# A gated product transposed in 32 x 32 blocks on VectorE and put in place by DMA copies, with three gate tiles ahead of the first branch

## The chip, the cores and the metric

The kernel runs on one core of one Trainium2 chip. The metric is device microseconds of one execution, the median of three runs. The engines are called PE (matrix products), DVE (VectorE), ACT (ScalarE), POOL (GpSimd) and SP (SyncE, which here only issues DMAs). ACT and POOL issue DMAs too; an engine that issues a DMA, or waits to issue it, does nothing else meanwhile.

## The reference

A decoder block on 512 tokens of 1024 channels in float32: two mixers side by side, merged by gates, then a feed-forward layer. Cut to what matters here:

```python
u, v_g, q, k, v, q_idx, k_idx, w_idx, gates = split_cols(h @ w_in, IN_SIZES)
y_a = gelu(u) * (einsum('gts,bcsgd->bctgd', tril(w_s), layernorm(gelu(v_g))) + b_s)   # 512 x 512
y_b = dsa_attention(rope(q), rope(k), v, ...)      # 8 heads of 64, the best 128 keys of each query
g = sigmoid(gates)                                 # 2 branches x 1024 channels
merged = g[0] * (y_a @ w_out_a) + g[1] * (y_b @ w_out_b)
x = x + merged @ w_o
x = x + square(relu(rmsnorm(x) @ w_ff_in)) @ w_ff_out
```

`y_a`, the gated product, comes out with tokens on the partitions. The product with `w_out_a` needs its channels there. That is the transposition of this change.

## The kernel before

**Products.** Each float32 product is three matmuls of a faster format: a value is split into a high half, which ACT writes (L51), and a low half, which DVE writes as the difference (L52; POOL for the weight tiles 3 to 23). `gemm` (L158 to L160) then multiplies low by high, high by low and high by high. A step of `gemm` is these three matmuls of 512 columns. One output tile of 128 channels takes 24 matmuls where the inner length is 1024, and 12 where it is 512.

**Weights.** Weight tiles of 512 KB are numbered in the order of use. Tile n arrives in `wr` (two buffers; loaded from SP's queue for n of 24 and more, L118), ACT makes `wh` of it and DVE `wl` (three buffers each). The load of tile n + 2 can start once `wl` of tile n is done. Tile 24 is that of gb0 before and after.

**Order.** The program collects steps of matmuls in a list `todo`, and `fill(n)` takes n of them to stand between work that has to wait for other engines. The scheduler then fixes the order on each engine. No instruction passes another on its engine.

**Around the change.** PE runs the k projection of the first four heads, the spatial gate `sg` (L575 to L577; DVE makes `u`, the gated product, from it at L578), the q projection `q0` in two tiles, one tile of the second gate `gb0`, and then the eight tiles `oa0` to `oa7` of the first branch, which are y_a times w_out_a. Among the last twelve matmuls of q0 stand 16 transposes of 128 x 128 by PE, in four groups `yt0` to `yt3`; ACT copies each group out as `yaTh` and DVE makes `yaTl`:

```python
b = bank(f"yt{g}", "pa")
for c in range(NT):
    tc.keep_in_program_order(PE.transpose(b[:, c * P:(c + 1) * P], u[:, c, g * P:(g + 1) * P], ident))
ACT.activation(yaT[0][:, g], b, AF.Copy)
DVE.tensor_tensor(yaT[1][:, g], b, f32(yaT[0][:, g]), op=ALU.subtract)
```

Meanwhile POOL issues the copies that put k, then q, head by head into `kq` (L368), 64 KB each; the heads' scores read them.

**Attention.** A head has four blocks of 128 queries. For each block PE makes the scores `at` (L639, L640); DVE masks and reduces them (L643); ACT takes exp (L646); DVE takes the reciprocal and normalises `p` (L651, L652); PE transposes it into `pt` (L658); ACT and DVE split that into `pth` and `ptl` (L661, L662). After the fourth block PE multiplies by the values, `pv` (L670). Between these steps `fill` puts branch tiles, k and q projections and gate tiles: `gb1` among the first heads, and `gb2` to `gb7` with the q projection among the last four. When these are used up, the scheduler takes matmuls of the second branch, `ob` (y_b times w_out_b), forward as far as the halves of y_b of the earlier heads allow. The evacuation of a gate tile, `zb`, is DVE's (L602).

Of the kernel before, what the change touches and what calls it, by code (L numbers as in the profile page):

```python
# [12 lines left out]
AF = mybir.ActivationFunctionType  # L13
ALU = mybir.AluOpType

P = 128
S = 512
D = 1024
KD = D // P
NT = S // P  # L20
# [13 lines left out]
def hybrid_block_kernel(ctx: ExitStack, tc: tile.TileContext, A: dict, out: bass.AP):  # L34
    nc = tc.nc
    ACT, DVE, POOL, PE = nc.scalar, nc.vector, nc.gpsimd, nc.tensor
# [7 lines left out]
    def bank(name, tag="ps"):  # L44
        return ps.tile([P, 512], F32, tag=tag, bufs=4, name=name)

    def f32(ap):
        return ap.bitcast(F32)

    def split(hi, lo, src, eng=None):  # L50
        ACT.activation(hi, src, AF.Copy)  # L51
        (eng or DVE).tensor_tensor(lo, src, f32(hi), op=ALU.subtract)  # L52


    def unit(tag, dt, name):
# [3 lines left out]
    def half(tag, bufs, name):  # L59
        pool, dt = (G, F32) if tag == "yb" else (E, FR)  # L60
        return pool.tile([P, 4, S], dt, tag=tag, bufs=bufs, name=name)
# [15 lines left out]
    todo, due = [], []  # L77
# [10 lines left out]
    def fill(n):  # L88
        while n > 0 and todo:
            try:  # L90
                next(todo[0])
                n -= 1
                tick()
            except StopIteration:
                todo.pop(0)
# [56 lines left out]
    def gemm(dst, get, ah, al, evac, lag=1, t0=0):  # L152

        wh, wl, n = get()
        K = len(ah)
        for k in range(K):
            bh, bl = ah[k][:, t0:], al[k][:, t0:]
            PE.matmul(dst, wl[:, k], bh, start=(k == 0), stop=False)  # L158
            PE.matmul(dst, wh[:, k], bl, start=False, stop=False)  # L159
            PE.matmul(dst, wh[:, k], bh, start=False, stop=(k == K - 1))  # L160
            if k == 0 and n is not None:
                w_ahead(n)
            if k == K - 1:
                later(evac, lag)
            yield

    def one(src):
        n = w_plan(src)

        def get():  # L170
            return *w_get(n, P), n
        return get
# [16 lines left out]
    hTh = [G.tile([P, S], FR, tag="hTh", bufs=KD, name=f"hTh{k}") for k in range(KD)]  # L189
    hTl = [G.tile([P, S], FR, tag="hTl", bufs=KD, name=f"hTl{k}") for k in range(KD)]  # L190
# [10 lines left out]
    ident = G.tile([P, P], F32, name="ident")  # L201
# [14 lines left out]
    W_GA = [one(A["wt"][12 + m]) for m in range(KD)]  # L216
    W_K0 = [one(A["wt"][n]) for n in (4, 5)]
    W_Q0 = [one(A["wt"][n]) for n in (8, 9)]
    W_GB = [one(A["wt"][20])]
    W_OA = [g for m in range(4) for g in pair(A["woa"][m])]  # L220
    W_GB += [one(A["wt"][21])]
    W_K1 = [one(A["wt"][n]) for n in (6, 7)]
    W_Q1 = [one(A["wt"][n]) for n in (10, 11)]
    W_GB += [one(A["wt"][20 + m]) for m in range(2, KD)]
    W_OB = [g for m in range(4) for g in pair(A["wob"][m])]
    W_O = [one(A["wo"][m]) for m in range(KD)]
    NG = 8
# [13 lines left out]
    for t in raw2:  # L241
        t = f32(t.rearrange("p a b -> p (a b)"))
        raw += [t[:, i * NA:(i + 1) * NA] for i in range(3)]
    hl = []
    for k in range(KD):
# [5 lines left out]
        elif k < 6:  # L251
            t = E.tile([P, 13, P], FR, tag="pt", bufs=2, name=f"wa{k}").rearrange("p a b -> p (a b)")
# [77 lines left out]
    for j in range(NT):  # L330
        rj = rstd[:, j:j + 1]
        for n in range(2):
            src = acc[j][n][:, :256].rearrange("p (h d) -> p h d", d=64)
# [7 lines left out]
    def rope(xy, T, name, t0):  # L341


        for n in range(2):
            a, b = tmp(f"{name}_a{n}")[:, t0:], tmp(f"{name}_b{n}")[:, t0:]
            DVE.tensor_tensor(a, xy[n], cosR[:, t0:], op=ALU.mult)
            DVE.tensor_tensor(b, xy[1 - n], sinR[:, t0:], op=ALU.mult)
            DVE.tensor_tensor(a, a, b, op=ALU.subtract if n == 0 else ALU.add)
            if name == "k0":
                DVE.tensor_copy(T[n], a)  # L350
                DVE.tensor_tensor(T[2 + n], a, f32(T[n]), op=ALU.subtract)
            else:
                split(T[n], T[2 + n], a)

    def rope_tiles(gets, name, done, t0=0):
        xy = [bank(f"{name}{n}")[:, t0:] for n in range(2)]

        def finish():
            t = [unit("T", FR, f"{name}_T{c}") for c in range(2)]
            T = [t[c][:, d, t0:] for c in range(2) for d in range(2)]  # L360
            rope(xy, T, name, t0)
            done(T)
        for n in range(2):
            yield from gemm(xy[n], gets[n], hTh, hTl, finish if n else (lambda: None), t0=t0)

    def restack(dst, T, hh, order, eng=nc.sync):
        for c, o in enumerate(order):
# [44 lines left out]
    for n in range(2):  # L412
        b = bank(f"kti{n}", "pa")
# [7 lines left out]
    u, vg = None, None  # L421
# [55 lines left out]
    mA, mAs = [], eight("mA")  # L477
# [90 lines left out]
    fill(12)  # L568
    u = dst_uv["u"]
    vgh, vgl = vghl  # L570
    yaT = [half("ybt", 2, f"yaT{c}") for c in "hl"]
    for g in range(4):
        b = bank(f"sg{g}", "pa")
        c = slice(g * P, (g + 1) * P)
# [4 lines left out]
                                 u[:, :, c], op0=ALU.add, op1=ALU.mult)  # L579
    fill(4)  # L580
    todo.append(rope_tiles(W_Q0, "q0", q_done))
    fill(11)
    for g in range(4):
        fill(1)
        b = bank(f"yt{g}", "pa")
        for c in range(NT):
            tc.keep_in_program_order(PE.transpose(b[:, c * P:(c + 1) * P], u[:, c, g * P:(g + 1) * P], ident))
        ACT.activation(yaT[0][:, g], b, AF.Copy)
        DVE.tensor_tensor(yaT[1][:, g], b, f32(yaT[0][:, g]), op=ALU.subtract)
    while todo:  # L590
        fill(8)

# [2 lines left out]
    def gate_b(m):  # L595
        b = bank(f"gb{m}")

        def evac():
            if m % 4 == 0:
                z1t.append(half("yb", 2, f"zb{m}"))  # L600
            z = z1t[-1][:, m % 4]
            DVE.tensor_tensor(z, b, R, op=ALU.mult)  # L602
            z1.append(z)
        yield from gemm(b, W_GB[m], hTh, hTl, evac)

    def branch_a(m):
        b = bank(f"oa{m}")

        def evac():
            DVE.tensor_tensor(mA[m], b, mA[m], op=ALU.mult)  # L610
        yield from gemm(b, W_OA[m], [yaT[0][:, k] for k in range(4)], [yaT[1][:, k] for k in range(4)], evac)


    todo.append(gate_b(0))
    for m in range(KD):
        todo.append(branch_a(m))
    fill(32)


    START = (0, 1, 2, 2)  # L620
# [82 lines left out]
                b.last = i == NT - 1  # L703
                advance(b, n)

    todo.append(gate_b(1))
    heads(0, (0, 1), (6, 7))
    todo.append(rope_tiles(W_K1, "k1", lambda T: ybs.__setitem__("KT", T)))
    heads(0, (2, 3), (6, 7))
# [5 lines left out]
    flush()  # L715
    k_done(ybs["KT"])
    todo.append(rope_tiles(W_Q1, "q1", q_done))
    todo.extend(gate_b(m) for m in range(2, KD))
    fill(27)
    heads(1, range(4), (2, 0))  # L720
    advance(None, (2, 2))
# [364 lines left out]
def _col_tiles(w, cols):  # L1086

    k = w.shape[0] // P
    t = w[:, cols].reshape(k, P, -1, P)
    return np.ascontiguousarray(t.transpose(2, 1, 0, 3)).reshape(-1, P, k * P)  # L1090
# [11 lines left out]
def _layout(x, norm1_g, w_in, w_s, b_s, sgu_ln_g, sgu_ln_b, w_out_a, w_out_b, w_o,  # L1102
            norm2_g, w_ff_in, w_ff_out, norm_f_g):
    c = np.ascontiguousarray
    x = np.asarray(x)[0]
    w = np.asarray(w_in)[0]
    cos, sin = _tables()
    k = KD
    a = {}
    a["xT"] = c(x.T.reshape(k, P, S).transpose(1, 0, 2))  # L1110
    a["xn"] = c(x.reshape(NT, P, D).transpose(1, 0, 2))
    g1 = np.asarray(norm1_g)[0].reshape(k, P).T
    a["x0"] = c(np.concatenate([g1, np.zeros_like(g1), a["xT"][:, 0]], axis=1))

    rows = np.arange(D).reshape(4, KD, 32).transpose(1, 0, 2).reshape(-1)
    a["xr"] = c(x.T[rows].reshape(k, P, S).transpose(1, 0, 2))
    a["g2"] = c(np.asarray(norm2_g)[0][rows].reshape(k, P).T)
    a["gf"] = c(np.asarray(norm_f_g).reshape(1, D))
    a["wa"] = c(np.concatenate([w[:, 2048:2560], w[:, 3072:3144]], axis=1).reshape(k, P, 584).transpose(1, 0, 2))
    cols = _rope_cols(2560) + _rope_cols(1536) + _rope_cols(1024) + list(range(3144, 5192))  # L1120
    a["wt"] = _col_tiles(w, cols)
    a["wuv"] = c(w[:, :1024].reshape(4, 2, P, 2, S).transpose(3, 0, 2, 1, 4)).reshape(8, P, 2 * S)
    a["ws"] = c(np.asarray(w_s)[0].transpose(2, 0, 1))
    a["bs"] = c(np.asarray(b_s)[0].T)
    a["lng"] = c(np.asarray(sgu_ln_g).reshape(1, S))
    a["lnb"] = c(np.asarray(sgu_ln_b).reshape(1, S))

    def pairs(t):
        n, p, f = t.shape
        return c(t.reshape(n // 2, 2, p, f).transpose(0, 2, 1, 3)).reshape(n // 2, p, 2 * f)  # L1130

    a["woa"] = pairs(_col_tiles(np.asarray(w_out_a)[0], slice(None)))
    a["wob"] = pairs(_col_tiles(np.asarray(w_out_b)[0], slice(None)))
    a["wo"] = _col_tiles(np.asarray(w_o)[0], rows)
    a["f1"] = _col_tiles(np.asarray(w_ff_in)[0][rows], slice(None))
    f2 = np.asarray(w_ff_out)[0].reshape(16, 2, P, 2, S)
    a["f2"] = c(f2[14:].transpose(0, 3, 2, 1, 4)).reshape(4, P, 2 * S)
    a["f2p"] = c(f2[:14].transpose(0, 2, 1, 3, 4)).reshape(14, P, 4 * S)
    a["cs"] = c(np.stack([np.tile(cos.T, (4, 1)), np.tile(sin.T, (4, 1))], axis=1))
    a["csn"] = c(np.stack([cos, sin]).reshape(2, NT, P, 32).transpose(2, 0, 1, 3))  # L1140
    return a
# [17 lines left out]
```

## Time and profile before

| | |
|---|---|
| median of three runs | 693.05 us (692.77, 693.05, 693.35) |
| the profiled execution: time / span | 693.35 / 691.6 us |
| PE busy | 683.3 us, 99% |
| DVE busy | 549.1 us, 79% |
| ACT busy | 341.0 us, 49% |
| POOL busy | 136.5 us, 20% |
| granted clock of PE, mean | 0.998 of full speed |

The span runs from the first to the last instruction. Matmuls overlap in PE's pipeline: the profile gives each a duration of 0.39 us for 512 columns, while the next one starts some 0.23 us after it. So a timeline of PE is read by starts.

### The profile page before, as it was taken

The numbers are of one execution on the slowest core, as the hardware profiler recorded it, in microseconds if no ns is written. First come the engines' busy times: TensorE is split into PE (matmuls) and PEld (weight loads), VectorE is DVE, ScalarE is ACT, GpSimd is POOL, SyncE is SP. The second block draws the span as 40 slices with busy tenths as digits, with TensorE's granted clock in tenths as the row PEclk, the third lists the DMA queues.
The fourth block names the chain that finished last, engine by engine and source line by source line (L and its number), as shares of the span: only waits on it lengthen the run. The fifth ranks groups of instructions, "written<-read, shape, count | busy, mean of one in ns | idle before, by whom it ended". The sixth has DMA issues, their size and how long they took to land.

```text
span 691.6 us, 8980 instructions
## 1 busy us (share of the span) xinstructions
PE 683.3 (99%) x3206; PEld 572.9 (83%) x3206; DVE 549.1 (79%) x1013; ACT 341.0 (49%) x593; POOL 136.5 (20%) x178
## 2 busy tenths in 40 slices
PE   8999999999999999999999999999999999999996
PEld 8998888888888888788888888888888888888885
DVE  5584999999767877878558756978788797878996
ACT  6644644432345545573337765357462645546143
POOL 0044347862730850000027000000000000000001
PEclk9999999999999999999999999999999999999999
DMA  8736232322951662224458332232333214133023
GB/s 322 254 112 194 66 98 83 102 91 62 252 144 62 160 171 67 104 79 136 138 185 234 100 122 91 78 137 61 126 118 122 69 66 171 61 122 123 0 62 121
DMA packets 26844, 84.12 MB, mean 122 GB/s; under 512 B 5168, under 2 KB 6832, under 8 KB 24752
## 3 DMA queue, kind: packets, MB, share of 16 engines
q1 hardware_dynamic: 16944, 48.38, 22.2%
q10 hardware_dynamic: 5760, 26.78, 11.2%
q0 software_dynamic: 4096, 8.40, 4.7%
q8 instruction: 25, 0.41, 0.2%
q14 instruction: 19, 0.16, 0.1%
HBM read 71.48 MB, written 2.10 MB: 106 GB/s over the span
## 4 chain that ended last, share of the span: by engine, by line
PE 97%; DMA 1%; DVE 0%; ACT 0%; issue 0%; SPq 0%; POOLq 0%; POOL 0%
PE f L159 8%; PE f L158 8%; PE f L160 8%; PE pp L917 6%; PE pp L918 6%; PE pp L919 6%; PE va L297 3%; PE gb L160 2%; PE gb L159 2%; PE gb L158 2%; PE wo L159 2%; PE ga L159 2%; PE ga L158 2%; PE wo L160 2%; PE wo L158 2%; PE ga L160 2%
## 5 line engine op out<-in xcount | busy, mean ns | idle before, releaser
L51 ACT ACTIVATE wh<-wr 128x1024 fp32r<-128x1024 f32 x88 | 92.7, 1055 | 74.6 <-issue 18.0
L52 DVE TENSOR_TENSOR wl<-wr,wh 128x1024 fp32r<-128x1024 f32 x67 | 81.3, 1216 | 30.4 <-ACT wh L51 30.4
L158 PE MATMUL f<-h2h,wl 128*128 128x512 f32 x256 | 99.6, 389 | 0.0
L159 PE MATMUL f<-h2l,wh 128*128 128x512 f32 x256 | 99.6, 389 | 0.0
L160 PE MATMUL f<-h2h,wh 128*128 128x512 f32 x256 | 99.6, 389 | 0.0
L51 ACT ACTIVATE u<-w2r 128x512 fp32r<-128x512 f32 x98 | 59.0, 626 | 74.7 <-DVE w2r L848 28.1
L918 PE MATMUL pp<-u,fp 128*128 128x512 f32 x196 | 76.2, 389 | 0.0
L919 PE MATMUL pp<-u,fp 128*128 128x512 f32 x196 | 76.2, 389 | 0.0
L52 DVE TENSOR_TENSOR u<-w2r,u 128x512 fp32r<-128x512 f32 x98 | 64.1, 684 | 11.3 <-ACT u L51 11.3
L917 PE MATMUL pp<-u,fp 128*128 128x512 f32 x196 | 72.0, 389 | 0.0
L929 DVE TENSOR_TENSOR P<-pp,P 128x512 f32<-128x512 f32 x84 | 54.4, 683 | 16.6 <-PE pp L919 16.6
L52 POOL TENSOR_TENSOR wl<-wr,wh 128x1024 fp32r<-128x1024 f32 x21 | 52.6, 2504 | 47.5 <-ACT wh L51 45.7
L1014 POOL TENSOR_TENSOR fss<-fss,mhalf 128x1 f32<-128x1 f32 x3 | 1.7, 557 | 302.3 <-DVE fss L1013 302.3
L158 PEld LDWEIGHTS f<-h2h,wl 128*128 128x128 f32 x256 | 48.1, 188 | 10.0
L160 PEld LDWEIGHTS f<-h2h,wh 128*128 128x128 f32 x256 | 48.1, 188 | 10.0
L159 PEld LDWEIGHTS f<-h2l,wh 128*128 128x128 f32 x256 | 48.1, 188 | 9.9
L876 ACT ACTIVATE fr<-f 128x512 f32<-128x512 f32 x32 | 19.1, 598 | 59.2 <-PE f L160 59.2
L917 PEld LDWEIGHTS pp<-u,fp 128*128 128x128 f32 x196 | 36.8, 188 | 7.7
L919 PEld LDWEIGHTS pp<-u,fp 128*128 128x128 f32 x196 | 36.8, 188 | 7.7
L918 PEld LDWEIGHTS pp<-u,fp 128*128 128x128 f32 x196 | 36.8, 188 | 7.6
L368 POOL DMA_DIRECT2D kq<-k_T x64 | 32.1, 509 | 46.9 <-ACT k_T L51 28.0
L813 POOL DMA_DIRECT2D acc<-x1B x32 | 17.0, 537 | 106.0 <-ACT h2h L781 100.0
(268 smaller groups left out, 1625.4 us busy)
## 6 DMA issues: line engine op xcount, KB each, us to landing
wr<-in_f SPq DMA_DIRECT2D x36, 512.0 KB, 3.5
w2r<-in_f2p ACTq DMA_DIRECT2D x14, 1024.0 KB, 5.0
wr<-in_wt SPq DMA_DIRECT2D x14, 512.0 KB, 4.3
wr<-in_wt ACTq DMA_DIRECT2D x14, 512.0 KB, 3.6
wr<-in_wuv ACTq DMA_DIRECT2D x8, 512.0 KB, 3.9
kq<-k_T POOLq DMA_DIRECT2D x64, 64.0 KB, 3.2
wr<-in_wo SPq DMA_DIRECT2D x8, 512.0 KB, 3.5
xn<-in_xn SPq DMA_DIRECT2D x2, 1024.0 KB, 8.4
```

What stands on the lines that cost most here:

```text
L51: ACT.activation(hi, src, AF.Copy)
L52: (eng or DVE).tensor_tensor(lo, src, f32(hi), op=ALU.subtract)
L158: PE.matmul(dst, wl[:, k], bh, start=(k == 0), stop=False)
L159: PE.matmul(dst, wh[:, k], bl, start=False, stop=False)
L160: PE.matmul(dst, wh[:, k], bh, start=False, stop=(k == K - 1))
L297: PE.matmul(acc[j][n][:, :CUT[n].stop - CUT[n].start], a[:, j * P:(j + 1) * P], b[:, CUT[n]], start=(k == 0 and q == 0), stop=(k == KD - 1 ...
L368: eng.dma_start(f32(dst[32 * c:32 * c + 32, :]), f32(T[o][32 * hh:32 * hh + 32, :]))
L876: ACT.activation(r, b, AF.Relu)
L917: PE.matmul(b[j], fl, u[:, 0], start=(q == 0), stop=False)
L918: PE.matmul(b[j], fh, u[:, 1], start=False, stop=False)
L919: PE.matmul(b[j], fh, u[:, 0], start=False, stop=(q == 1))
L929: DVE.tensor_tensor(sums[name, j], b[j], sums[name, j], op=ALU.add)
```

## The change

The 16 transposes by PE go. DVE transposes `u` in 32 x 32 blocks in four instructions (L589 of the changed kernel) into `uB`; in it every block is transposed, but a channel's blocks still lie in other partitions than the product wants. 16 copies of 32 partitions by 2 KB, 64 KB each, from SBUF to SBUF put them in place as `yaR` (L595): eight are issued by SP and eight by ACT, in turn. ACT and DVE then split `yaR` into the halves `yaT` (four tiles each). Tokens and channels stand in another order in these than before, so the first branch reads its moving operand in four runs of 128, its evacuation reads PSUM in runs of 32, and the rows of `w_out_a` are permuted on the host.

The order of the work changes too: three gate tiles, gb0 to gb2, stand between q0 and oa0 instead of one; gb1 leaves the first heads and gb2 the last ones. The weights' order follows. The second tile of q0 is roped two steps behind its last matmul instead of one, and ACT's high halves of q0 keep the program's order.

```diff
     def split(hi, lo, src, eng=None):
-        ACT.activation(hi, src, AF.Copy)
+        first = ACT.activation(hi, src, AF.Copy)
         (eng or DVE).tensor_tensor(lo, src, f32(hi), op=ALU.subtract)
+        return first
...
-    W_GB = [one(A["wt"][20])]
+    W_GB = [one(A["wt"][20 + m]) for m in range(3)]
     W_OA = [g for m in range(4) for g in pair(A["woa"][m])]
-    W_GB += [one(A["wt"][21])]
...
-    W_GB += [one(A["wt"][20 + m]) for m in range(2, KD)]
+    W_GB += [one(A["wt"][20 + m]) for m in range(3, KD)]
...
-                split(T[n], T[2 + n], a)
+                hi = split(T[n], T[2 + n], a)
+                if name == "q0":
+                    tc.keep_in_program_order(hi)
...
-            yield from gemm(xy[n], gets[n], hTh, hTl, finish if n else (lambda: None), t0=t0)
+            yield from gemm(xy[n], gets[n], hTh, hTl, finish if n else (lambda: None), 2 if name == "q0" else 1, t0)
...
-    yaT = [half("ybt", 2, f"yaT{c}") for c in "hl"]
...
-    fill(11)
-    for g in range(4):
-        fill(1)
-        b = bank(f"yt{g}", "pa")
-        for c in range(NT):
-            tc.keep_in_program_order(PE.transpose(b[:, c * P:(c + 1) * P], u[:, c, g * P:(g + 1) * P], ident))
-        ACT.activation(yaT[0][:, g], b, AF.Copy)
-        DVE.tensor_tensor(yaT[1][:, g], b, f32(yaT[0][:, g]), op=ALU.subtract)
+    fill(2)
+    uB = f32(half("ybt", 2, "uB"))
+    for c in range(NT):
+        tc.keep_in_program_order(DVE.transpose(
+            uB.rearrange("p q (b c e) -> p (q b) c e", c=NT, e=32)[:, :, c],
+            u[:, c].rearrange("p (b e) -> p b e", e=32)))
+    yaR = half("yb", 2, "yaR")
+    for a in range(4):
+        for q in range(4):
+            (nc.scalar if q % 2 else nc.sync).dma_start(yaR[32 * q:32 * q + 32, a], uB[32 * a:32 * a + 32, q])
...
-            DVE.tensor_tensor(mA[m], b, mA[m], op=ALU.mult)
-        yield from gemm(b, W_OA[m], [yaT[0][:, k] for k in range(4)], [yaT[1][:, k] for k in range(4)], evac)
-    todo.append(gate_b(0))
+            z = mA[m].rearrange("p (c a e) -> p c a e", c=NT, a=4)
+            DVE.tensor_tensor(z, b.rearrange("p (a c e) -> p c a e", a=4, c=NT), z, op=ALU.mult)
+        yield from gemm(b.rearrange("p (a t) -> p a t", a=4), W_OA[m], yaT[0], yaT[1], evac)
+    todo.extend(gate_b(m) for m in range(3))
+    fill(12)
+    yaT = [half("ybt", 2, f"yaT{c}") for c in "hl"]
+    for a in range(4):
+        split(yaT[0][:, a], yaT[1][:, a], yaR[:, a])
+    yaT = [[t.rearrange("p a (g t) -> p g a t", g=4)[:, g] for g in range(4)] for t in yaT]
     for m in range(KD):
         todo.append(branch_a(m))
-    fill(32)
+    fill(23)
...
-    todo.append(gate_b(1))
     heads(0, (0, 1), (6, 7))
...
-    todo.extend(gate_b(m) for m in range(2, KD))
+    todo.extend(gate_b(m) for m in range(3, KD))
```

The host permutes the rows of `w_out_a` with `arange(S).reshape(4, 4, 32).transpose(1, 0, 2)`.

The order of instructions on three engines, at the places where it differs most. A name is a tile with its number; `<-` stands between what is written and what is read.

DVE, from the last of k's rope on, before (k0 and q0 are the first halves of k and q, wl24 and wl25 low halves of weight tiles):

```order
L52 TENSOR_TENSOR wl24_1638<-wr24_1509,wh24_1637 128x1024
L351 TENSOR_TENSOR k0_T1_1585<-k0_a1_1593,k0_T0_1584 128x512
L346 TENSOR_TENSOR q0_a0_1724<-q00_1632,cosR_86 128x512
L52 TENSOR_TENSOR wl25_1668<-wr25_1539,wh25_1667 128x1024
L589 TENSOR_TENSOR yaTl_1551<-yt0_1682,yaTh_1550 128x512
```

DVE at the same place, after:

```order
L52 TENSOR_TENSOR wl24_1636<-wr24_1509,wh24_1635 128x1024
L351 TENSOR_TENSOR k0_T1_1583<-k0_a1_1591,k0_T0_1582 128x512
L589 STREAM_TRANSPOSE uB_1644<-u_967 128x16x32 x4
L52 TENSOR_TENSOR wl25_1688<-wr25_1539,wh25_1687 128x1024
L346 TENSOR_TENSOR q0_a0_1726<-q00_1630,cosR_86 128x512
L347 TENSOR_TENSOR q0_b0_1727<-q01_1631,sinR_87 128x512
```

The four block transposes stand where the first instruction of q's rope stood, behind wl24 and ahead of wl25; the subtractions of yaTl are gone from there.

ACT from wh25 to wh27, before:

```order
L51 ACTIVATE wh25_1667<-wr25_1539 128x1024
L588 ACTIVATE yaTh_1550<-yt0_1682 128x512
L588 ACTIVATE yaTh_1550<-yt1_1692 128x512
L588 ACTIVATE yaTh_1550<-yt2_1702 128x512
L588 ACTIVATE yaTh_1550<-yt3_1712 128x512
L51 ACTIVATE wh26_1758<-wr26_1641 128x1024
L51 ACTIVATE q0_T0_1722<-q0_a0_1724 128x512
L51 ACTIVATE q0_T0_1722<-q0_a1_1731 128x512
L51 ACTIVATE wh27_1791<-wr27_1671 128x1024
```

ACT at the same place, after (L595 are the copies that ACT issues):

```order
L51 ACTIVATE wh25_1687<-wr25_1539 128x1024
L595 DMA yaR_1649<-uB_1644 32x512 x8
L51 ACTIVATE wh26_1718<-wr26_1639 128x1024
L51 ACTIVATE q0_T0_1724<-q0_a0_1726 128x512
L51 ACTIVATE q0_T0_1724<-q0_a1_1733 128x512
L51 ACTIVATE yaTh_1798<-yaR_1649 128x512 x3
L51 ACTIVATE wh27_1783<-wr27_1691 128x1024
L51 ACTIVATE yaTh_1798<-yaR_1649 128x512
```

Eight copies now stand ahead of wh26, and the four high halves of the gated product behind it. wh26 belonged to the first two oa tiles before, and belongs to gb2 after.

PE at the end of the last head (head 7, its blocks 2 and 3), before:

```order
L658 MATMUL pt7_2_2892<-ident_95,p7_2_2840 128x128 x3
L160 MATMUL ob1_2949<-ybsh_2192,wh40_2750 128x512
L158 MATMUL ob3_3003<-ybsh_2192,wl41_2853 128x512
L159 MATMUL ob3_3003<-ybsl_2193,wh41_2852 128x512
...
L658 MATMUL pt7_3_2904<-ident_95,p7_3_2867 128x128 x4
L159 MATMUL ob3_3003<-ybsl_2193,wh41_2852 128x512
...
L158 MATMUL ob5_3045<-ybsh_2192,wl42_2938 128x512
L159 MATMUL ob5_3045<-ybsl_2193,wh42_2937 128x512
L670 MATMUL pv7_2915<-ptl_1890,VS0_80 128x512
```

PE at the same place, after, from the last scores at7_3 on:

```order
L652 MATMUL at7_3_2888<-kq11_2359 128x512
L159 MATMUL ob5_3047<-ybsh_2226,wl42_2940 128x512
L670 MATMUL pt7_1_2897<-ident_95,p7_1_2840 128x128 x2
L160 MATMUL ob5_3047<-ybsl_2227,wh42_2939 128x512
...
L161 MATMUL ob5_3047<-ybsh_2226,wh42_2939 128x512
L670 MATMUL pt7_2_2904<-ident_95,p7_2_2874 128x128 x3
L670 MATMUL pt7_3_2910<-ident_95,p7_3_2891 128x128 x4
L682 MATMUL pv7_2917<-ptl_1904,VS0_80 128x512
```

Before, 26 matmuls of gate and second branch lie between at7_3 and pv7; after, six do, all ahead of pt7_2. The first scores of head 0 stand 33 matmuls behind the first of oa0, against 72 before.

## Rows read from the trace of the kernel before

**Rows 1.** The page's busy times and its chain by engine, and PE's waits in the whole span (engine, line and tile; releaser; us in total, times, longest).

```profile
PE 683.3 (99%) x3206; PEld 572.9 (83%) x3206; DVE 549.1 (79%) x1013; ACT 341.0 (49%) x593; POOL 136.5 (20%) x178
PE 97%; DMA 1%; DVE 0%; ACT 0%; issue 0%; SPq 0%; POOLq 0%; POOL 0%
PE va L301 <- DVE wah L278: 1.5, 1, 1.5
PE va L297 <- DVE wal L52: 0.3, 1, 0.3
```

**Rows 2.** PE's timeline around the transposes (start us, duration us, instruction).

```profile
166.22 0.39 PE L160 MATMUL q<-hTh,wh 128*128 128x512 f32 x1
...
166.90 0.39 PE L160 MATMUL q<-hTh,wh 128*128 128x512 f32 x1
167.13 0.60 PE L587 MATMUL yt<-ident,u 128*128 128x128 f32 x4
...
171.67 0.40 PE L158 MATMUL gb<-hTh,wl 128*128 128x512 f32 x1
```

**Rows 3.** The chain of waits from 164 to 174 us (start us, us, piece).

```profile
167.29 0.44 PE yt L587 x4
167.73 0.23 PE q L158
...
170.70 0.44 PE yt L587 x4
```

**Rows 4.** The tile sg (duration in ns: min, median, max; first and last start; form).

```profile
L575 PE MATMUL sg<-vgl,ws x4: 389/389/389, 153.5 to 155.6; 128*128 128x512 f32 x4
```

**Rows 5.** DVE's timeline at the end of q0.

```profile
169.15 1.21 DVE L52 TENSOR_TENSOR wl<-wr,wh 128x1024 fp32r<-128x1024 f32 x1
170.28 0.67 DVE L351 TENSOR_TENSOR k_T<-k_a,k_T 128x512 fp32r<-128x512 f32 x1
170.89 0.67 DVE L346 TENSOR_TENSOR q_a<-q,cosR 128x512 f32<-128x512 f32 x1
```

**Rows 6.** The tile x1B, which DVE transposes in 32 x 32 blocks later in the kernel.

```profile
L783 DVE STREAM_TRANSPOSE x1B<-xr x8: 711/712/714, 320.8 to 356.6; 128x512 f32<-128x512 f32 x8
```

**Rows 7.** Copies and loads. First the tile QSi, whose copies of 32 partitions SP issues, with the time from issue to landing; then the DMA issues from 160 to 195 us (KB each, median us to landing); then the tile kq from 172 to 176 us.

```profile
L368 SPq DMA_DIRECT2D QSi<-qi_T x32: 507/588/1366, 44.3 to 66.2; - x32
DMA to landing us min/median/max: 1.9/3.0/4.6
...
kq<-k_T POOLq DMA_DIRECT2D x32, 64.0 KB, 4.0
wr<-in_woa SPq DMA_DIRECT2D x3, 512.0 KB, 4.7
...
L368 POOL DMA_DIRECT2D kq<-k_T x7: 498/498/498, 171.7 to 175.5; - x7
DMA to landing us min/median/max: 3.7/4.8/5.4
```

**Rows 8.** ACT's timeline: wh26.

```profile
175.04 1.06 ACT L51 ACTIVATE wh<-wr 128x1024 fp32r<-128x1024 f32 x1 [3.27 <-DMA wr<-in_woa]
```

**Rows 9.** Stretches of the span: busy us (and count) of each engine, PE's granted clock, the DMA engines' mean busy share and GB/s.

```profile
core 0: us, PE busy (x) PEld busy (x) DVE busy (x) ACT busy (x) POOL busy (x), PEclk, DMA share, GB/s
172.00:174.00 2.00, 2.00 (x11) 1.64 (x10) 2.00 (x4) 0.00 (x0) 2.00 (x5) 1.00 0.90 324
174.00:176.00 2.00, 2.00 (x11) 1.65 (x9) 2.00 (x4) 0.96 (x1) 1.15 (x3) 1.00 1.00 217
...
172.00:190.00 18.00, 18.00 (x81) 14.91 (x80) 14.28 (x21) 5.40 (x6) 14.52 (x31) 1.00 0.91 250
```

**Rows 10.** PE's timeline at the end of the last head.

```profile
286.79 0.40 PE L640 MATMUL at<-kq 128*128 128x512 f32 x1
...
288.69 0.39 PE L158 MATMUL ob<-ybsh,wl 128*128 128x512 f32 x1
...
292.01 0.60 PE L658 MATMUL pt<-ident,p 128*128 128x128 f32 x4
...
294.08 0.91 PE L670 MATMUL pv<-ptl,VS 128*128 128x512 f32 x4
```

**Rows 11.** DVE's timeline there.

```profile
287.93 0.67 DVE L643 CUSTOM_DVE_ANT_0 p<-at,sc 128x512 f32<-128x512 f32 x1
...
288.93 0.40 DVE L652 TENSOR_SCALAR p<-p,s 128x384 f32<-128x384 f32 x1
289.26 0.67 DVE L602 TENSOR_TENSOR zb<-gb,R 128x512 f32<-128x512 f32 x1
...
290.00 0.16 DVE L651 RECIPROCAL s<-s 128x1 f32<-128x1 f32 x1
...
291.21 0.48 DVE L652 TENSOR_SCALAR p<-p,s 128x512 f32<-128x512 f32 x1
...
293.34 0.69 DVE L662 TENSOR_TENSOR ptl<-pt,pth 128x512 fp32r<-128x512 f32 x1 [1.18 <-ACT pth L661]
```

**Rows 12.** ACT's timeline there.

```profile
288.20 1.06 ACT L51 ACTIVATE wh<-wr 128x1024 fp32r<-128x1024 f32 x1
289.17 0.71 ACT L646 ACTIVATE p<-p,s 128x512 f32<-128x512 f32 x1
289.78 0.19 ACT L646 ACTIVATION_READ_ACCUMULATOR p<-p,s 128x1 f32 x1
```

More of the change, by code (lines that the diff above doesn't have):

```diff
@@ L1130, in pairs @@
         return c(t.reshape(n // 2, 2, p, f).transpose(0, 2, 1, 3)).reshape(n // 2, p, 2 * f)
-    a["woa"] = pairs(_col_tiles(np.asarray(w_out_a)[0], slice(None)))
+    ya_rows = np.arange(S).reshape(4, 4, 32).transpose(1, 0, 2).reshape(-1)
+    a["woa"] = pairs(_col_tiles(np.asarray(w_out_a)[0][ya_rows], slice(None)))
     a["wob"] = pairs(_col_tiles(np.asarray(w_out_b)[0], slice(None)))
```

## The prediction

> **What bounds the kernel now.** I read the page's engine shares first, then the chain that ended last, then PE's waits. PE is busy for 99% of the span and holds 97% of the chain; in all the span it waits twice, 1.5 and 0.3 us, both in an earlier stage, where v is projected [rows 1]. Its clock is the full one [rows 9]. So an instruction taken off PE shortens the kernel by what PE spent on it, and a wait put on PE lengthens it by its whole length, unless a later wait takes it up; behind the two places of this change there is none to do so. On DVE (79% busy), ACT (49%) and the DMA queues a cost counts only where PE comes to wait for it. The views to read are therefore PE's timeline at the two places, and beside it those of DVE and ACT, to see how long before PE's need each operand is ready.
>
> **What is removed: 16 transposes on PE.** The first starts at 167.13 and the first gate tile gb0 at 171.67, 4.54 us later; between them stand the transposes and 12 matmuls [rows 2]. At the pitch of plain matmuls, three in 0.68 or 0.227 each [rows 2], the 12 take 2.72, which leaves **1.82 us** for the transposes. The chain gives 0.44 for each four, 1.76 [rows 3], the rest being slower neighbours. With them go four copies on ACT and four subtractions on DVE from PSUM; their like comes back as the split of yaR, off the chain.
> The Trainium skill speaks against such an exchange: the page "VectorE: DVE Perf Modes", section "Rules for kernel authors", says to transpose 128 by 128 on TensorE where PSUM will do as destination, and its section "The three transpose paths" gives 390 ns for one there. By that figure, an estimate, the change would take 16 x 0.39 = 6.2 us off PE and come out near 691. The row shows why it would not: pipelined, four cost 0.44.
>
> **What is moved: two gate tiles to the front.** gb1 and gb2, 48 matmuls, now stand between gb0 and the first branch. They are the same work, so nothing in itself. gb1 was a filler of the first heads anyway; gb2, 24 matmuls or 5.4 us, was one of the fillers of the last heads. The new moving operand of oa is read in four runs of 128; the sg matmuls read theirs in that form at 389 ns each, as the plain ones of [rows 2] do [rows 4], so nothing. The evacuation of oa in runs of 32 goes to DVE, which has time there; the host's permutation costs nothing.
>
> **Front, gb0.** With the transposes gone PE is through q0 at 171.67 - 1.82 = 169.85. gb0 needs the low half of weight tile 24, which DVE ends at 169.15 + 1.21 = 170.36 [rows 5]; DVE's instructions up to it stand in the same row as before, back to back. So PE waits **0.55** with the handover. One third of the gain is lost at once, and gb0 starts at 170.40.
>
> **Front, gb1.** DVE does its four block transposes from 170.89, where q_a stood [rows 5]. One of the same shape takes 0.712 [rows 6]; four follow one another in 2.7, to 173.6. wl25 behind them ends at 174.8; gb1 is due at 170.40 + 24 x 0.227 = 175.8. No wait, and the q rope behind it has no taker before 187.
>
> **Front, gb2: the copies.** All 16 read all four blocks, so they start at 173.6, 8 on SP and 8 on ACT. Behind ACT's eight stands wh26 [the ACT rows of the change], behind that on DVE wl26, behind that on PE gb2; behind SP's eight the load of wr27. The nearest row for an issue is SP's copies of 32 partitions, 0.588 each [rows 7]. The fifth copy of each queue waits until the first has landed. With landing L, ACT's last ends at 173.6 + L + 4 x 0.59 = 175.95 + L; wh26 takes 1.06 [rows 8], wl26 1.21, so gb2's operand is ready at 178.25 + L with a little handover, and gb2 is due at 170.40 + 48 x 0.227 = 181.28. The wait is L - 3.0. For L the rows give 3.0 (SP's copies in an emptier stretch), 4.0 (POOL's copies of the same 64 KB in this stretch) and up to 5.4 for those issued between 172 and 176 [rows 7], when the DMA engines are 0.9 to 1.0 busy [rows 9]. I take 4.0, the same size in the same stretch: **1.0**, between 0 and 2.4.
> The page "DMA: Bandwidth & Descriptors", section "Issuing engines are not separate DMA queues", of the Trainium skill says that transfers of all issuing engines share the same 16 DMA engines and that a second issuer saves only issue time. By it the upper end of L would be the nearer and gb2 would wait some 2 us; no row of before shows SP, ACT and POOL copying together.
>
> **Front, oa0 and the first scores.** gb2 then runs from 182.3 to 187.7. wr27 is issued at about 180.0 and lands in 4.7 [rows 7]; wh27 at 184.7, wl27 ready at 187.0; the planes of yaT by 187.6, the last of them needed only nine matmuls into oa0. **Nothing**, since the wait at gb2 covers it; if L is 3.0 about 0.2. The first scores stand 33 matmuls behind oa0's start, at 195.2; their q copies on POOL start once q_T's low half is done, about 190.6, and land by 195. Nothing, but up to 1.0 if the 1 MB of copies pushes POOL's back.
>
> **The tail: the cover that is gone.** Before, 26 fillers lie between the last scores at7_3 and pv7, and pt7_2, pt7_3 stand among them [the PE rows of the change, rows 10]. Now six are left, with nothing between pt7_2, pt7_3 and pv7; the other matmuls follow pv7 or were done earlier. That is gate tile gb2, spent at the front. The steps between them are softmax, and they set the time:
> - pt7_2 could go at 288.69, but its normalise ends at 288.93 + 0.40 = 289.33 [rows 11]: 0.64. Its three transposes, at three quarters of the 0.44 for four, end at 289.66.
> - pt7_3 needs exp, reciprocal and normalise of 7_3. The score is done at 288.60 [rows 11]; exp now follows at once, since wh42 no longer stands ahead of it on ACT (before it started at 289.17 [rows 12]); with its accumulator 0.8, the reciprocal 0.1 and the normalise 0.48 [rows 11], it is ready at 290.08: 0.42.
> - From pt7_3 to pv7 before: 292.01 to 294.08, 2.07 [rows 10], and pv7 came right behind DVE's ptl at 293.34 + 0.69 = 294.03 [rows 11]: this chain had no slack. PE now has only the four transposes to do in it, 0.44: 1.63.
> Together **2.7**, from 2.4 (the first step met by a DVE that is freer, the gate's evacuation no longer on it) to 3.1. Behind pv7 both orders are alike.
>
> **Sum.** -1.82 + 0.55 + 1.0 + 0 + 2.7 = +2.43. The profiled execution took 693.35, so 695.8; the median of the runs, 693.05, is 0.3 below it, so **695.5**. With both ends of the unknown terms (gb2 0 to 2.4, tail 2.4 to 3.1, scores 0 to 1) it is 694.2 to 697.9 on the scale of the median.
>
> **Rivals.**
> 1. The tail costs its least and the copies land in 3.0: -1.82 + 0.55 + 2.4 = +1.1, or **694.2**, the waits just eating the gain. For it: SP's copies show a median of 3.0. Against it: that was not beside POOL's copies.
> 2. The copies are late, L 5.4, and push back POOL's q copies: -1.82 + 0.55 + 2.4 + 1.0 + 2.7 = +4.8, or **697.9**. For it: a mean DMA share of 0.91 between 172 and 190 [rows 9], and 1 MB more in it. Against it: wr27's load, 512 KB, leaves just that stretch.
> 3. Faster: the transposes' 1.82 is kept because the tail is not paid. Place: pt7_3 to pv7. If head 7's scores were done 2.7 us ahead of PE, the softmax chain would run beside earlier matmuls and PE would find its operands; with L below 3 the result is 693.05 - 1.82 = **691.2**, or 691.8 with the wait for wl24. It decides if all waits together stay below 0.4. For it: DVE and ACT lose work in the last heads (one gate tile's evacuation, an earlier wh42). Against it: at7_3 itself is PE's, 20 matmuls nearer to pv7, and the chain of 2.07 starts only after it.
> 4. The transposes' place on PE is empty but PE was not at its limit there, so that nothing is gained: 1.82 more, **697.3**. PE's timeline without a gap speaks against it [rows 2].
>
> **How the numbers follow.** Forecast (694.5 to 697) 0.56; rival 1 0.19; rival 2 0.14; rival 3 0.07; rival 4 0.04. A measurement of this kernel can tell about 0.2%, 1.39 us, from no change: faster is below 691.66, slower above 694.44. Rival 3 alone is faster: 0.07. Rival 1 is within: 0.19, and I put a little of the forecast's low edge there: 0.21. Slower has the rest, 0.72. The range from 693.7 to 697.6 leaves out rival 3, most of rival 2 and the edge of rival 1.
>
> **What would show it.** PE's waits of the changed kernel: about 0.5 before the first gb matmul (releaser DVE wl), about 1 at the third gate tile (DVE wl, behind ACT's copies), and three in the tail: before pt (DVE p, twice) and before pv (DVE ptl), 2.7 together. The first step is wrong if gb0 starts where q0 ends; the second if the copies' median landing is under 3 or over 5; the third if pv7 starts less than 2 us behind pt7_3 or if PE has a filler there after all. The forecast as a whole is wrong if the tail's waits stay under 1.5, or if the scores of the first head wait for their copies by more than 1.

## The result, and the profile after

The changed kernel takes 701.74 us (median of four runs, 700.01 to 702.27) against 693.05 us: ratio 1.0121, 95% interval 1.0109 to 1.0133. It is slower, as forecast, but by 8.7 us and not by 2.4, and outside the range. The profiled execution took 701.22 us, 7.87 more than that of before.

The page, the chain by engine (answers to [rows 1]):

```profile
PE 81%; DVE 14%; DMA 2%; issue 1%; ACT 1%; SPq 0%; POOLq 0%; ACTq 0%; POOL 0%; DVEq 0%
```

The chain has left PE for 19% of the span. What PE waits for now, beyond the two waits that it had (engine, line and tile; releaser; us in total, times, longest):

```profile
PE gb L159 <- DVE wl L52: 3.2, 2, 2.8
PE pv L682 <- DVE ptl L674: 1.5, 1, 1.5
PE pt L670 <- ACT p L658: 0.6, 1, 0.6
PE pt L670 <- DVE p L664: 0.3, 1, 0.3
```

These are the places and the releasers that the prediction named (it gave DVE for the 0.6), 5.6 us together where it had 4.25. Less the 1.82 of the transposes, that is 3.8 and not 7.9. PE's timeline of the front (start us, duration us) shows where the rest is; it answers to [rows 2]:

```profile
169.48 0.39 PE L161 MATMUL q<-hTh,wh 128*128 128x512 f32 x1
170.28 0.50 PE L159 MATMUL gb<-hTh,wl 128*128 128x512 f32 x1 [0.41 <-DVE wl L52]
...
181.06 0.39 PE L161 MATMUL gb<-hTh,wh 128*128 128x512 f32 x1
184.26 0.50 PE L159 MATMUL gb<-hTh,wl 128*128 128x512 f32 x1 [2.82 <-DVE wl L52]
...
185.87 0.63 PE L159 MATMUL gb<-hTh,wl 128*128 128x512 f32 x1
186.29 0.63 PE L160 MATMUL gb<-hTl,wh 128*128 128x512 f32 x1
...
191.49 0.39 PE L159 MATMUL oa<-yaTh,wl 128*128 128x512 f32 x1
```

From 185.87 on the matmuls start 0.42 apart, not 0.227, until about 189. The tail shows the same, behind pv7 (answers to [rows 10]):

```profile
295.79 0.40 PE L652 MATMUL at<-kq 128*128 128x512 f32 x1
...
298.48 0.52 PE L670 MATMUL pt<-ident,p 128*128 128x128 f32 x3 [0.63 <-ACT p L658]
299.32 0.63 PE L670 MATMUL pt<-ident,p 128*128 128x128 f32 x4 [0.32 <-DVE p L664]
301.42 1.36 PE L682 MATMUL pv<-ptl,VS 128*128 128x512 f32 x4 [1.47 <-DVE ptl L674]
...
303.75 0.63 PE L159 MATMUL ob<-ybsh,wl 128*128 128x512 f32 x1
...
305.29 0.40 PE L160 MATMUL ob<-ybsl,wh 128*128 128x512 f32 x1
```

Stretches of both places say why (busy us and count of each engine; granted clock, DMA share and GB/s at the end). The granted clock is 0.50 there, 1.2 GHz; it was 1.00 in every stretch of before that I read [rows 9]:

```profile
187.00:188.00 1.00, 1.00 (x3) 0.72 (x3) 0.67 (x2) 0.00 (x0) 0.00 (x0) 0.50 0.90 295
...
303.00:305.00 2.00, 2.00 (x7) 1.73 (x6) 0.39 (x1) 0.59 (x1) 0.00 (x0) 0.50 0.00 0
```

The difference of the two profiled executions, from PE's starts:

| from, to | before | after | difference |
|---|---|---|---|
| start of gb0 | 171.67 | 170.28 | -1.39 |
| gb0 to gb2, 48 matmuls | 10.90 (at 0.227) | 13.98 | +3.08 |
| gb2 to oa0, 24 matmuls | 5.45 (at 0.227) | 7.23 | +1.78 |
| at7_3 to pv7 | 7.29, less 20 fillers (4.54) | 5.63 | +2.88 |
| pv7 to the fifth ob behind it | 2.33 | 3.87 | +1.54 |

Together 7.89, the 7.87 that was to be explained. The second and the fourth row are waits; the third and the fifth are the lower clock, 3.3 us, with some 0.1 of a slow first matmul in the third.

Why gb2's operand was late: the chain of waits between the transposes and gb2 (start us, us, piece; answers to [rows 5, 8]).

```profile
173.25 0.60 ACTq L595
...
173.89 4.21 DMA yaR<-uB
...
178.11 3.79 DMA yaR<-uB
...
181.90 1.06 ACT wh L51
...
182.98 1.24 DVE wl L52
```

The tile yaR, which the 16 copies write, with the time from issue to landing (answers to [rows 7]):

```profile
DMA to landing us min/median/max: 3.6/4.2/5.3
```

A landing took 4.2 us, near the 4.0 that I took. But the eight copies kept ACT from 173.25 to 181.77. Its queue shows where that time went (ACT's fifth and sixth copy together, then the seventh, then the eighth):

```profile
177.40 1.27 ACTq L595 DMA_DIRECT2D yaR<-uB  x2
178.71 1.31 ACTq L595 DMA_DIRECT2D yaR<-uB  x1
180.07 1.71 ACTq L595 DMA_DIRECT2D yaR<-uB  x1
```

The fifth copy started when the first, issued at 173.25, had landed after 4.1 us: the one wait that the prediction had. From there to the end of the eighth's issue it took 4.37 us, where the prediction had four issues of 0.59, 2.36. The sixth waited another 0.2, for the second copy; the seventh and the eighth started behind the landings of the third and the fourth (178.5 and 179.7) and waited for none, but their issues took 1.31 and 1.71. The 3.79 that the chain above puts to a landing is therefore none: the copy issued at 178.11 took 4.4 us, to 182.5, when wh26 was already running. hold_gate7, below, has the same front, and in it ACT waited for no landing at all: the fourth copy's issue ended at 176.65, when the first, issued at 172.89, had landed after 3.1. The eight issues alone took 9.21 us there:

```profile
172.89 9.21 ACTq L595 DMA_DIRECT2D yaR<-uB  x8
```

Tile 27, which oa0 needs, was late as well. SP issued its load at 181.47, behind its own eight copies, and it took 7.2 us to land; ACT's wh27 had to wait for it:

```profile
188.81 1.06 ACT L51 ACTIVATE wh<-wr 128x1024 fp32r<-128x1024 f32 x1 [3.25 <-DMA wr<-in_woa]
```

DVE finished wl27 at 189.90 + 1.23 = 191.13, just ahead of oa0's start at 191.49.

### The profile page after: what moved, and what is told of

Same layout as the page of the kernel before. It is cut to its first block, busy times and chain, and to the rows that moved or that the text cites. A ratio compares the mean times of both kernels' runs of the same rounds, so it can differ in the third digit from the quotient of the medians.

```text
span 699.5 us, 8981 instructions
## 1 busy us (share of the span) xinstructions
PE 685.4 (98%) x3190; PEld 573.1 (82%) x3190; DVE 551.7 (79%) x1017; ACT 341.1 (49%) x593; POOL 136.5 (20%) x178
## 4 chain that ended last, share of the span: by engine, by line
PE 81%; DVE 14%; DMA 2%; issue 1%; ACT 1%; SPq 0%; POOLq 0%; ACTq 0%; POOL 0%; DVEq 0%
PE f L159 8%; PE f L160 8%; PE f L161 8%; PE pp L928 6%; PE pp L930 6%; PE pp L929 6%; DVE sc L541 4%; PE va L297 3%; DVE m L539 3%; PE wo L159 2%; PE wo L160 2%; PE wo L161 2%; PE gb L159 2%; PE gb L161 2%; PE pv L682 2%; PE gb L160 2%
```

## The experiments

Each time stands against runs of the kernel before on the same chip.

**gates_only.** Three gates in front, the first scores 33 matmuls behind oa0, but the transposition as before:

```diff
-    DVE.transpose(...) x4, 16 copies into yaR, split of yaR
+    PE.transpose(...) x16 into yt, ACT and DVE make yaT of it, as in the kernel before
```

> Three gate tiles stand in front as in the changed kernel, but PE transposes the gated product as before, with no copies and no block transposes. My theory (the tail's wait comes of the moved gate tiles alone, 2.9 us of waits on pt7_2, pt7_3 and pv7, and the clock falls behind them for another 1.5): 693.05 + 4.4 = 697.4, no wait at the third gate tile, granted clock at 0.5 for some 3.5 us behind pv7. Rival (the late copies push the heads back and the tail's wait is only their echo): no wait in the tail, about 693.

Measured: 696.22 us (695.23 to 697.61) against 692.71, ratio 1.0051 (1.0035 to 1.0066). PE's waits:

```profile
PE pv L674 <- DVE ptl L666: 1.5, 1, 1.5
PE pt L662 <- ACT p L650: 0.6, 1, 0.6
PE pt L662 <- DVE p L656: 0.3, 1, 0.3
```

The stretch around pv7, with the granted clock third from the end:

```profile
295.00:305.00 10.00, 8.53 (x42) 6.73 (x41) 5.23 (x9) 6.39 (x11) 0.00 (x0) 1.00 0.09 28
```

The tail's three waits are there to a tenth without any copy: they belong to the moved gate tiles, and the rival falls. The clock did not fall in the profiled execution, which took 695.23, 2.5 over before; so the waits alone account for it. The other executions go up to 697.6: the mean granted clock was 0.998 in the two at 695.2 and 695.5 and 0.996 in the two at 696.9 and 697.6. As far as these means tell, the lower clock that my theory added came in two executions of four.

**wh26_first.** wh26 ahead of ACT's last four copies:

```diff
+    fill(1)                                  # gb0's first step makes wh26
+    with tc.issue_after(<wh26>):
+        copies of the planes a = 2, 3
```

> The changed kernel with the high half of weight tile 26 put on ACT ahead of its last four copies; SP's queue is left as it is. My theory (two operands are late behind the copies, not one): gb2 finds its operand, but oa0 then waits for weight tile 27, whose load stands behind SP's eight copies and lands at 188.8, so oa0 still starts near 191 and the clock falls there instead: 700 to 702. Rival (ACT's blocked queue is the whole price of the front): the wait of 2.8 and the clock's 1.8 behind it go, about 697.

Measured: 703.33 us against 692.71, ratio 1.0154 (1.0138 to 1.0169). PE's timeline, its two waits at oa0:

```profile
191.86 0.80 PE L159 MATMUL oa<-yaTh,wl 128*128 128x512 f32 x1 [4.89 <-ACT yaTh L51]
...
193.74 0.79 PE L160 MATMUL oa<-yaTl,wh 128*128 128x512 f32 x1 [1.09 <-DVE yaTl L52]
```

gb2 no longer waits, so it was wh26's place behind ACT's copies that held it; and oa0 starts where it did, at 191.86 against 191.49. But the edit moved more than ACT's queue. SP's last four copies stand behind wh26 too, and SP's loads went in among them:

```profile
177.75 0.33 SPq L119 DMA_DIRECT2D wr<-in_woa  x1
...
185.03 1.14 SPq L626 DMA_DIRECT2D yaR<-uB  x2
```

The load is that of tile 27, issued 3.7 us earlier than in the changed kernel; the last copy landed at 191.1, where in the changed kernel it landed at 185.4. So here the last plane of the product was late and not tile 27, and the edit itself made it so. The run shows that gb2's wait can go without any time won, as long as another operand holds oa0. The rival as it was meant, with SP's queue left alone, was not run; what speaks against it is keep_warm, which comes next.

**keep_warm.** Matmuls that nobody reads, put where PE waits, into the bank that the next matmul overwrites:

```diff
+    def warm(b, n):
+        for _ in range(n):
+            tc.keep_in_program_order(PE.matmul(b, hTh[0][:, :P], hTh[1], start=True, stop=True))
+    # 12 before gb2, 2 before pt7_2, 1 before pt7_3, 6 before pv7
```

> The changed kernel with matmuls whose results nobody reads, put where PE waits: 12 ahead of gb2 (2.7 us), 2 ahead of pt7_2, 1 ahead of pt7_3, 6 ahead of pv7. My theory (behind each wait PE runs at the lower clock, which costs 1.8 and 1.5 us on top of the waits): the operands come as late as before, but the granted clock stays at 1.00 and 3.3 us come back: 698.3. Rival (the slow matmuls behind the waits are slow for another reason, as DMA traffic into SBUF): the extra matmuls change nothing or add to the time, 701.5 to 703.

Measured: 699.38 us against 692.71, ratio 1.0096 (1.0079 to 1.0113), 2.4 less than the changed kernel (2.0 if each is set against its own runs of before), with more work on PE. A stretch behind each filled wait:

```profile
184.00:190.00 6.00, 4.78 (x22) 3.61 (x20) 2.90 (x4) 1.91 (x3) 2.25 (x5) 1.00 0.89 257
...
299.00:305.00 6.00, 6.00 (x29) 4.68 (x28) 2.22 (x4) 2.83 (x4) 0.00 (x0) 1.00 0.01 3
```

PE's one new wait:

```profile
PE oa L159 <- DVE wl L52: 1.6, 1, 1.6
```

The clock holds at 1.00 with the DMA share still at 0.89, so the slow matmuls were the clock's and not the DMA's. 2.0 to 2.4 and not 3.3 came back. From at7_3 to the eleventh ob behind it (the fifth ob behind pv7 in the changed kernel) PE now took 7.68 us and not 9.50: the tail's part came back. The front's did not: from gb2 to oa0 it still took 7.19 against 7.23, because PE, faster now, came to oa0 before the low half of tile 27. That wait of 1.6 lay under the lower clock in the changed kernel. So ACT's queue is not the whole price of the front, and the two causes there, the clock and the late tile 27, are not to be added: each alone would hold oa0 about as long.

**hold_gate7.** The last gate tile behind the last scores:

```diff
-    todo.extend(gate_b(m) for m in range(3, KD))
+    todo.extend(gate_b(m) for m in range(3, KD - 1))
...
+            if blk.h == 7 and blk.last:
+                with tc.issue_after(<at7_3>):
+                    run(gate_b(7))
```

> The changed kernel with the last gate tile, gb7, held back until the last scores at7_3 are issued, so that 24 matmuls lie between them and pv7 again. My theory (heads 4 to 7 have slack on DVE and ACT, so PE can do without these fillers earlier): the tail's waits and the lower clock behind them go, 701.5 - 4.4 = 697.1, no new wait. Rival (the cover is only moved): a wait of about the same length among heads 4 to 7, 700 to 702.

Measured: 708.57 us against 692.71, ratio 1.0225 (1.0209 to 1.024). My theory falls, and further than the rival said. PE's timeline, some of its new waits:

```profile
283.13 0.92 PE L682 MATMUL pv<-ptl,VS 128*128 128x512 f32 x4 [2.08 <-DVE ptl L674]
...
288.45 0.87 PE L670 MATMUL pt<-ident,p 128*128 128x128 f32 x3 [1.51 <-DVE p L664]
...
290.76 1.09 PE L670 MATMUL pt<-ident,p 128*128 128x128 f32 x4 [1.02 <-DVE p L664]
293.32 1.54 PE L682 MATMUL pv<-ptl,VS 128*128 128x512 f32 x4 [1.47 <-DVE ptl L674]
```

The last heads have no slack: a filler held back for the end of head 7 is missing in the heads before it, where it brings two groups of waits in place of one. The second group has its lower clock too: 0.50 from 290 to 298 us.

**early_two_gates and early_three_gates.** The block transposes directly behind u, wl24 ahead of k's rope, the copies behind wh25; POOL's copies in another order; two or three gates in front, the first scores 96 matmuls behind q0 in both; k0 is roped one step later:

```diff
+    for c in range(NT): DVE.transpose(uB..., u[:, c]...)     # right behind the loop over sg
     fill(4)
     todo.append(rope_tiles(W_Q0, "q0", q0_done))
-    fill(2)
+    fill(9)
+    with tc.issue_after(<wh25>):
+        the 16 copies
...
+            with tc.issue_after(<wl24>):
+                rope(xy, T, "k0", t0)
...
+    POOL: k's high halves of four heads, low k of heads 0 and 1, q of heads 0 and 1, then the others
...
-    todo.extend(gate_b(m) for m in range(3))                 # early_two_gates only
+    todo.extend(gate_b(m) for m in range(2))
```

early_two_gates also splits yaR ahead of wh26.

> DVE transposes the blocks right behind the gated product, ahead of k's rope, with the low half of tile 24 behind them; the copies are issued right behind wh25, while the DMA engines are little used; two gate tiles stand in front and gb2 is back among the last heads, the first scores 96 matmuls behind q0 as before. So that the later k rope does not hold up the first scores, POOL copies k's high halves first and the first two heads' q ahead of the other heads' low k. My theory (the front's waits come of the copies' late start, the tail's of the third gate tile): no wait in the tail, at most 0.6 at oa0, 693.05 - 1.82 + 0.6 = 691.8. Rival (the copies delay k, q and the first scores wherever they stand): a wait of 2 to 4 us before the first scores and the lower clock behind it, 695 to 698.

> As early_two_gates, but with gb2 in front as in the changed kernel; the first scores stand 96 matmuls behind q0 here too (the changed kernel has 105). My theory (it is the third gate tile, taken from the last heads, that uncovers the tail): the front is free of waits, the tail has its 2.4 to 2.9 and behind it up to 1.5 of lower clock: 693.05 - 1.82 + 2.9 to 4.4 = 694.1 to 695.6. Rival (the tail's wait comes of the first scores standing 9 matmuls later): no wait in the tail, 691.3.

Measured: early_two_gates 698.67 us, ratio 1.0081 (1.0067 to 1.0095); early_three_gates 695.14 us (693.91 to 696.26), ratio 1.0028 (1.0019 to 1.0037), both against 693.11. PE's one new wait in early_two_gates, in its timeline:

```profile
185.75 0.77 PE L159 MATMUL oa<-yaTh,wl 128*128 128x512 f32 x1 [4.96 <-DVE wl L52]
```

What PE waits for in early_three_gates, but for the two waits that before has too:

```profile
PE pv L702 <- DVE ptl L694: 1.5, 1, 1.5
PE pt L690 <- ACT p L678: 0.6, 1, 0.6
PE pt L690 <- DVE p L684: 0.3, 1, 0.3
```

The stretch of its tail:

```profile
293.00:305.00 12.00, 10.42 (x37) 8.59 (x38) 4.49 (x8) 6.72 (x10) 0.00 (x0) 0.72 0.07 23
```

With three gates the front is free of waits and the tail has its 2.4 and the lower clock; with two the tail is free and oa0 waits. The first scores stand at the same place in both, so the tail's wait is the price of the third gate tile, not of the later scores: theory right, rival out. early_two_gates missed theory and rival alike: the wait is at oa0 and not before the first scores, 5.0 and not 0.6, since ACT was 10 us at issuing its eight copies (166.65 to 176.64, half of it waits for landings) and the last landed at 181.7.

**copy_order_only.** The kernel before with nothing but POOL's new order of copies:

```diff
-    k_done: for each head, its high and low k; then q_done: q of all heads
+    k's high halves of four heads, low k of heads 0 and 1, q of heads 0 and 1, low k and q of heads 2 and 3
```

> The kernel before with nothing changed but POOL's order of copies, as in the two kernels above (high halves of k first, q of the first two heads ahead of the low k of the other two). My theory: PE waits for none of these copies there, so 693.05, within 0.2%. Rival (the copies' order is worth something by itself): below 691.7.

Measured: 692.71 us against 693.11, ratio 0.9998 (0.9989 to 1.0007): no change. What the two early kernels show does not come of this order of copies. The two kernels that follow bring q of head 0 further forward still; that order was not run by itself.

**three_queues.** early_two_gates with the copies on three queues and the low half in place; POOL copies q of head 0 right behind k of head 0:

```diff
-    (nc.scalar if q % 2 else nc.sync).dma_start(...)
+    (nc.sync, nc.scalar, nc.gpsimd)[(4 * a + q) % 3].dma_start(...)
...
-    yaT = [half("ybt", 2, f"yaT{c}") for c in "hl"]
+    yaT = [half("ybt", 2, "yaTh"), yaR.bitcast(FR)]
```

> early_two_gates with two things changed so that the operands of oa0 are there sooner: the 16 copies go to three queues (six on SP, five on ACT, five on POOL, which is idle until k's halves are done), and the low half of the product is written over yaR and not into the place of uB, so that it needn't wait until all copies have read uB. POOL copies q of head 0 right behind k of head 0. My theory (with the transposition through early enough, two gate tiles cover it and the last heads keep all their fillers): no wait at oa0 or in the tail, 693.05 - 1.82 = 691.2, up to 691.9 with a short wait. Rival (SP's and ACT's shared completion semaphores and the loads between the copies hold them up whatever the queue): oa0 waits 2 us or more and the clock falls, 695 to 698.

Measured: 698.69 us against 693.0, ratio 1.0076 (1.0062 to 1.009). The rival's signs came, a wait at oa0 and the lower clock behind it (0.50 from 186 to 190 us); its 695 to 698 fell just short. PE's one new wait, and the chain of waits from the copies on:

```profile
PE oa L159 <- ACT q_T L51: 4.5, 1, 4.5
...
168.81 6.29 DMA yaR<-uB
...
175.12 0.52 ACTq L617
...
175.68 5.22 DMA yaR<-uB
```

SP issued the load of tile 26, 512 KB, at 168.25; its copy issued behind that, at 168.81, took 6.29 to land, and ACT's last two copies stood waiting for it. ACT's high half of q, which the profile names, stands behind them and behind wh26 on ACT. The load is not the whole reason. From issue to landing, the copies being issued between 168.9 and 169.5 us, in early_two_gates, which has the same load at 168.22, and then in three_queues:

```profile
DMA to landing us min/median/max: 3.6/3.8/3.9
...
DMA to landing us min/median/max: 5.9/6.1/6.3
```

Behind the same load, copies took 3.6 to 3.9 on two queues and 5.9 to 6.3 on three, ACT's and POOL's as well as SP's. Why they were slower on three is not shown.

**loads_behind_copies.** The same with the loads of tiles 26 and 27 behind SP's copies. The expectation calls this one order changed; the edit also turns the queues round, so that ACT issues six copies and SP five:

```diff
-(nc.sync, nc.scalar, nc.gpsimd)[(4 * a + q) % 3].dma_start(...)
+(nc.scalar, nc.gpsimd, nc.sync)[(4 * a + q) % 3].dma_start(...)
...
             state["c"] += 1
-            w_load()
+            if n not in (24, 25):
+                w_load()
...
+    with tc.issue_after(<SP's last copy>):
+        w_load()
+        w_load()
```

> three_queues with one order changed: the loads of weight tiles 26 and 27 are issued on SP behind its share of the copies, not between them. My theory (in three_queues the copies issued behind the 512 KB load of tile 26 landed after 6 us instead of 2, and ACT's last copy waited for one of them): all copies land by about 174, ACT is free by 171, no wait at oa0, 691.2 to 691.9. Rival (the copies are slow by their own number and size, whatever is queued ahead of them): a landing time of 5 us or more again, a wait at oa0 of 3 us or more, 696 to 698.

Measured: 691.04 us (690.8 to 691.57) against 692.94, ratio 0.9974 (0.9963 to 0.9986). It beats both kernels. All that PE waits for in the whole span:

```profile
PE va L302 <- DVE wah L279: 1.5, 1, 1.5
```

The tile yaR, from issue to landing:

```profile
DMA to landing us min/median/max: 2.1/3.1/4.6
```

No wait is left that was not there before. The gain of 1.9 us (1.0 to 2.6 by the interval) agrees with the 1.82 of the transposes. Between 168.9 and 169.5 us, where three_queues had 5.9 to 6.3, the copies landed in 2.7 to 3.3, with no load ahead of them; the 4.6 are of ACT's last three, issued behind the load of tile 26. What the turned queues did by themselves is not shown.

## Why the prediction was wrong

- **The transposes, -1.82:** right. gb0 started 1.39 earlier, which is 1.82 less its wait, and some 0.1 from an earlier stage; loads_behind_copies shows the whole of it.
- **gb0, 0.55:** right; 0.41 of idle time and a slow first matmul.
- **gb1, no wait:** right. DVE's four block transposes took 2.5 us.
- **gb2, 1.0:** the place, the releaser and the wait for the first landing were right, the size was not: 2.8 of wait, 3.08 with the slow start. L was 4.2, and L - 3.0 would have given 1.2. The step that failed is "173.6 + L + 4 x 0.59": the last four issues took 4.37 and not 2.36, so that ACT was free at 181.8 and not at 180.0, although the copies could start 0.35 earlier than reckoned. 0.588 is the median of [rows 7], from another stretch; the same row has an issue of 1.366. The sign set for this step, a median landing under 3 or over 5, could not see it. Why the issues took so long stays open.
- **oa0 and the first scores, nothing:** right in the number, by luck. Tile 27's load was issued 1.5 us later than reckoned and landed in 7.2, not 4.7, so its low half was done at 191.1 and not at 187.0. oa0 did not wait because gb2's wait and the lower clock had pushed it back to 191.5: one miss covered the other. In keep_warm, without the lower clock, the wait shows, 1.6.
- **The tail, 2.7:** right. 2.4 of idle time, 2.88 by starts; all three waits, and their cause in the third gate tile, shown by gates_only and by the pair of early kernels.
- **What was missing: PE's clock.** The sum has no term for it and the rivals none either; it stood at nothing without a reason. It took 1.78 and 1.54 in the profiled execution, as much as a wait each; in the front most of the 1.78 would otherwise have been a wait at oa0, as keep_warm shows. The page "TensorE: Matmul & The Clock Gate" of the Trainium skill, section "Part 1: The HAM clock gate", says that PE falls to its lower clock after it has been idle; I didn't bring it in. The trace agrees: 0.50 granted behind both waits. But the same three waits in the tail left it at 1.00 in the profiled execution of gates_only.
- **The range:** its own terms add up to 698.3 at the upper end (-1.82 + 0.55 + 2.4 + 3.1 + 1.0 = +5.2), not 697.9. The result lies above either.

So of the 5.4 us that the sum lacks (7.87 against 2.43), 3.3 are the clock and 2.1 the wait at gb2, which the slow issues account for. The third rival's time, 691.2, was reached in loads_behind_copies. What it took was not scores ahead of PE, as that rival had it, but a transposition early enough to need two gates only.

## What to carry to other kernels

A filler taken from one latency-bound stage to cover another is not free even if PE never waited: hold_gate7 shows that where the stage has no slack, the wait comes back, and longer (3.6 us at pv and 3.5 at pt, in place of 1.5 and 0.9). Before PE is relieved by a path of copies, find the last instruction that is queued behind their issue on each engine, and price every issue, not only the first landing: a row from another stretch had 0.59 for what took 1.31 and 1.71 here. Look further down each queue too: the next weight tile's load stood behind SP's copies. If a forecast puts a wait of some microseconds on PE at its full clock, reckon the matmuls behind it at the lower clock as a second case.

## What the runs showed of the hardware that I had not expected

- The lower clock is not the same in each execution. gates_only and early_three_gates have the same three waits in the tail, yet in the profiled executions the clock was 1.00 behind them in the one and 0.72 on the mean (293 to 305 us) in the other. Their times spread over 2.4 us each, where loads_behind_copies, without these waits, spreads over 0.8.
- More queues did not speed the copies. On two queues they landed in 3.6 us (median, early_two_gates; 5.9 at most), on three in 5.2 (6.3), both with a 512 KB load issued among them, and in 3.1 (4.6) on the same three queues with the loads behind SP's share.
- An issue of a 64 KB copy took ACT between 0.5 and 1.7 us in the changed kernel, in one queue and within 9 us.
- What stands behind an issue on its engine waits, but an instruction already begun goes on: in wh26_first ACT's wh26 ran from 176.82 to 177.88 while ACT issued a copy at 177.10.
